# Seven-product pairs that add in one PSUM bank, and 2048-column low parts

## The chip, the cores and the metric

The kernel runs on one core of a Trainium2 chip. The metric is the device time of one execution, in microseconds, as the median over runs. TensorE does the matmuls; VectorE (DVE), ScalarE (ACT) and GpSimd (POOL) do elementwise work; SyncE (SP) issues the loads of weights. Matmul results go to PSUM, which the kernel uses as eight banks of 128 x 512 float32; everything else lives in SBUF.

## The reference

A trunk of two layers for one sequence of 256 tokens, width 1024, in float32. Cut to what matters here:

```python
def hybrid_layer(h, p_i, ...):
    u = rms_norm(h, g_mix_pre)
    (..., gate_a, gate_b) = jnp.split(u @ w_in, offsets, axis=-1)
    branch_a = (o_gla * jax.nn.silu(gg)) @ w_o_gla        # gated linear attention
    branch_b = gqa_attention(q, k, v) @ w_o_attn          # grouped-query attention
    mixed = jax.nn.sigmoid(gate_a) * branch_a + jax.nn.sigmoid(gate_b) * branch_b
    h = h + rms_norm(mixed @ w_out, g_mix_post)

    gate, up = jnp.split(rms_norm(h, g_ffn_pre) @ w_ffn_in, 2, axis=-1)      # 1024 -> 2 x 2816
    h = h + rms_norm((jax.nn.silu(gate) * up) @ w_ffn_out, g_ffn_post)       # 2816 -> 1024

    e = p_i @ w_ple_proj
    return h + rms_norm(jax.nn.sigmoid(h @ w_ple_gate) * e, g_ple_post)
```

## The kernel before

**Precision.** A float32 number is held as a high part and a low part, and each product is made of three matmul passes: high by high, low by high, high by low. `passes` orders them (line 120): for weights as the moving operand it first runs the passes with the high weights for all four blocks of 128 rows, then the four with the low weights. `mm3` (line 104 in the profile) runs the three passes one after the other, so that its second matmul already needs the low weights. A product of 128 tokens by 512 columns over 512 rows is 12 matmuls.

**Weights.** All weights stream from HBM in an order written out beforehand (`plan`), in units of mostly 128 x 2048 float32, 1 MB. `Stream` loads a unit into a raw buffer (two of them, `rawp`; SyncE issues the load at line 294), copies it on ScalarE into the high part `wh` (line 132, in two pieces of 1024 columns) and subtracts that on VectorE from the raw to get the low part `wl` (line 128, in two pieces, each behind its own copy). There are four slots (`wp`) for finished units. `take` hands the next one to the step that uses it; `done` frees it, and `fill` makes the next job's unit.

**Pairs with seven products.** Where a unit of tokens by weights is a 2 x 2 block product (two halves of rows, two of columns), the kernel uses the seven-product form of Strassen and Winograd instead of eight. Per layer there are four such pairs: one in the gate stage (`seven` with `gate_b`) and three in the FFN stage (`pair`, for the blocks `PAIRS`). The sums of the weight blocks are formed in place in lent weight slots: `Stream.step` holds seven steps for a pair, makes a unit at each, and adds two raw blocks at four of them (lines 324, 327, 330, 335, each one 128 x 2048 add on VectorE). x is the running sum in a lent slot, z another lent slot, y a large buffer, q an ordinary raw buffer. `sums` forms the matching sums of the tokens. `seven` (lines 608 to 649) runs the products, `times` each of them, with a `then` behind it that evacuates PSUM: ScalarE copies at lines 635, 638 and 642, a subtract through `vsub` (line 128), and three adds (line 615) once the fifth product is there. Each product except the first two accumulators takes a fresh PSUM bank.

**Order.** The order of a stage is a string. In the gate stage `GATES` mixes u (a unit of the other gate) and m (a unit of an output projection) with the digits of the pair's steps; in the FFN stage `FFN` mixes u (a plain block, `block`), o (a unit of the second FFN matrix, `out_step`) and digits:

```python
FFN = "uu12u34u5u67" "uo12o34o5o67" "poo12o345o67"
GATES = "uuu1u2m34m5m67m"
```

A pair's result is gated, multiplied, and transposed by TensorE some steps later (`turned`, a queue of tasks that count ticks; transposes appear at line 439). Three outs remain for the end of the FFN stage (the stage's tail), where they are run for each half of the tokens. Inside these orders a scheduler places each engine's instructions.

Of the kernel before, what the change touches and what calls it, by code (L numbers as in the profile page):

```python
# [10 lines left out]
F32 = mybir.dt.float32  # L11
# [3 lines left out]
ALU = mybir.AluOpType  # L15
# [43 lines left out]
def trunk_kernel(ctx: ExitStack, tc: tile.TileContext, a: dict, out: bass.AP):  # L59
# [106 lines left out]
    def unit(w, kh, c0):  # L166

        return lambda t: [
            (
                t[:, :2048].rearrange("p (k c) -> p k c", c=512),  # L170
                w[kh * 512 : (kh + 1) * 512, c0 : c0 + 512].rearrange("(k p) c -> p k c", p=P),
            )
        ]
# [25 lines left out]
            )  # L199
        ]  # L200

    plan = []
    for l in range(DEPTH):
        w = a["w_in"][l]
        plan += [unit_rows(w, n, C_RA, C_RA + 1056, FIRST if l + n == 0 else None) for n in range(4)]
        for c0 in (C_AK, C_GQ, C_GK, C_GV, C_GV + 512, C_GG, C_GG + 512):
            plan += [unit(w, kh, c0) for kh in range(2)]
        by_block = lambda w, c: [unit(w, kh, c + j * 512) for j in range(2) for kh in range(2)]
        gates, merges = by_block(w, C_GA), by_block(a["w_o_gla"][l], 0)
        pair = [unit(w, kh, C_GB + j * 512) for kh in range(2) for j in range(2)]  # L210
        for x in GATES:
            plan.append(gates.pop(0) if x == "u" else merges.pop(0) if x == "m" else (pair, int(x)))
        plan += by_block(a["w_o_attn"][l], 0)
        plan += [unit(a["w_out"][l], kh, j * 512) for kh in range(2) for j in range(2)]
        if l == 0:
            plan += [unit_rows(a["w_ple_proj"][l], 0)]
        w = a["w_ffn_in"][l]
        blocks = [[unit_gate_up(w, kh, b) for kh in range(2)] for b in range(NBLK)]
        plan += blocks[0] + blocks[1]
        plains = [u for b in PLAIN for u in blocks[b]]  # L220
        pairs = [[unit(w, kh, c + b * 256) for kh in range(2) for c in (0, HIDDEN)] for b in PAIRS]
        outs = [unit_rows(a["w_ffn_out"][l], n) for n in OUT]
        for x in FFN.replace("p", ""):
            if x == "1":
                pair = pairs.pop(0)
            plan.append(plains.pop(0) if x == "u" else outs.pop(0) if x == "o" else (pair, int(x)))
        plan += outs
        plan += [unit(a["w_ple_gate"][l], kh, j * 512) for kh in range(2) for j in range(2)]
        if l + 1 < DEPTH:
            plan += [unit_rows(a["w_ple_proj"][l + 1], 0)]  # L230

    class Load:


        def __init__(self, make, own=None, waits=False):
            self.make, self.own, self.waits, self.raw, self.n = make, own, waits, None, 0

        def start(self):
            if self.own:
# [5 lines left out]
    class Stream:  # L245
# [8 lines left out]
        def __init__(self, depth):  # L254
            self.depth, self.held, self.room, self.ready, self.open = depth, 0, 0, [], False
            self.loads, self.jobs, self.lend = [], [], False
            pairs = {}
            for item in plan:
                if callable(item):
                    x = Load(item)  # L260
                    self.loads.append(x)
                    self.jobs.append(lambda x=x: self.plain(x))
                else:
                    units, n = item
                    if n == 1:
                        b11, b12, b21, b22 = units
                        x, z = (Load(b, lambda tag=tag: self.lent(tag), tag == "wh") for b, tag in ((b11, "wh"), (b12, "wl")))
                        y, q = Load(b22, big), Load(b21)
                        pairs[id(units)] = x, y, z, q
                        self.loads += [x, y, z]  # L270
                    if n == 5:
                        self.loads.append(q)
                    self.jobs.append(lambda p=pairs[id(units)], n=n: self.step(n, *p))

# [36 lines left out]
            return self.jobs.pop(0)()  # L311

        def plain(self, x):
            return self.put(x)

        def made(self, x):
            for piece in self.put(x):
                split(*piece)

        def step(self, n, x, y, z, q):  # L320
            c = slice(0, 2048)
            if n == 1:
                self.made(x)
                nc.vector.tensor_tensor(out=x.raw[:, c], in0=x.raw[:, c], in1=z.raw[:, c], op=ALU.add)
            elif n == 2:
                self.made(y)
                nc.vector.tensor_tensor(out=z.raw[:, c], in0=z.raw[:, c], in1=y.raw[:, c], op=ALU.add)
            elif n == 3:
                self.made(x)
                nc.vector.tensor_tensor(out=x.raw[:, c], in0=x.raw[:, c], in1=y.raw[:, c], op=ALU.add)  # L330
            elif n == 4:
                self.made(z)
            elif n == 5:
                self.made(x)
                nc.vector.tensor_tensor(out=x.raw[:, c], in0=x.raw[:, c], in1=q.raw[:, c], op=ALU.add)
            elif n == 6:
                self.made(q)
            else:
                self.load()
                self.made(x)  # L340
                self.held -= 1
                self.lend = True

        def fill(self):
            while self.open and self.held < self.depth and self.jobs:
# [259 lines left out]

        return made, Task(make(), part[0])

    def seven(sp, forms, gated):

        made, task = forms  # L610
        quad = lambda hf, j: lambda k: sp.tok(4 * j + k, hf)
        form = lambda i: lambda k: [p[:, k, :] for p in made[i]]

        def add(out, x, y):
            nc.vector.tensor_tensor(out=out, in0=x, in1=y, op=ALU.add)

        (p1, v), (p3, p7) = (halves(mid()) for _ in range(2))
        c11, p5, o = acc(), acc(), []
        c12, c22 = p3, p7

        def product(i, then):

            o[:] = [acc()]
            times(o[0], form(i), True, then)

        def both():
            add(v, o[0], v)
            add(c12, v, p3)
            add(c22, v, p7)

        def last():
            vsub(v, p5, c22)
            gated(1, v, c22)

        times(c11, quad(0, 0), True, lambda: nc.scalar.copy(p1, c11))
        yield
        task.need()
        product(0, lambda: nc.scalar.copy(p3, o[0]))
        yield
        times(p5, form(1), True, lambda: vsub(v, p5, p1))  # L640
        yield
        product(2, lambda: nc.scalar.copy(p7, o[0]))
        yield
        product(3, both)
        yield
        times(c11, quad(0, 1), False, lambda: gated(0, c11, c12))
        yield
        times(p5, quad(1, 1), False, last)
        yield

    def project_t(sp):
# [232 lines left out]
    for l in range(DEPTH):  # L884
# [404 lines left out]
        def sigmoid(br, hf, j, src):  # L1289
            if sgate[br] is None:  # L1290
                sgate[br] = big().rearrange("p (s c) -> p s c", s=2)
            with tc.issue_after(last_exp[0].ins):
                nc.scalar.activation(sgate[br][:, hf, j * 512 : (j + 1) * 512], src, AF.Sigmoid)

        def blocks(sp, then):

            for j in range(2):
                o = [acc(), acc()]
                for kh in range(2):
                    w = ws.take()  # L1300
                    for hf in range(2):
                        amode(o[hf], sp, hf, kh * 4, w, kh == 0, kh == 1)
                    if kh == 1:
                        for hf in range(2):
                            then(j, hf, o[hf])
                    ws.done()
                    yield
# [16 lines left out]
        def merge(br):  # L1324
# [15 lines left out]
        steps = {  # L1340
            "u": blocks(uT, lambda j, hf, o: sigmoid(0, hf, j, o)),
            "m": blocks(gT, merge(0)),
            "s": seven(uT, forms, gate_b),
        }
        for x in GATES:
            if x == "m":
# [44 lines left out]
        for hf in range(2):  # L1391
            ws.lend = hf == 1
            for b in range(2):
                o = acc()
                for kh in range(2):
                    amode(o, u2, hf, kh * 4, us[b][kh], kh == 0, kh == 1, fresh=b == 0)
                sg = t512()
                nc.scalar.activation(sg[:, 0:256], o[:, 0:256], AF.Silu)
                vmul(sg[:, 0:256], o[:, 256:512], sg[:, 0:256])
                turned(sg[:, 0:256], 2 * b, 2, hf)  # L1400
                if hf == 1:
                    ws.done(2)
                if (hf, b) == (1, 0):
                    forms = sums(plain)
# [32 lines left out]
        def pair(b):  # L1437
            def gated(hf, gate, up):
                sg = t512()
                nc.scalar.activation(sg, gate, AF.Silu)  # L1440
                vmul(sg, up, sg)
                turned(sg, 2 * b, 4, hf, WAIT_LAST[hf] if b == PAIRS[-1] else WAIT_PAIR)

            return seven(u2, forms, gated)

        o = []

# [135 lines left out]
```

## Time and profile before

| | |
|---|---|
| median of 3 runs | 924.27 us (923.92 to 924.66) |
| profiled execution, first to last instruction | 922.9 us |
| matmuls and transposes on TensorE | busy 912.2 us, 99%, 4668 records |
| weight loads on TensorE | busy 776.2 us, 84% |
| VectorE | busy 786.1 us, 85%, 1002 instructions |
| ScalarE | busy 578.5 us, 63%, 954 instructions |
| GpSimd | busy 83.8 us, 9% |
| HBM read | 169.50 MB; 187 GB/s over the span |

The runs' time stands 1.4 us above the profiled span (924.27 - 922.9). In the profile, PE is the matmul part of TensorE, PEld its weight loads, L with a number a line of the kernel, and names such as `acc_0ffnin` a tile of layer 0's FFN stage. An entry "2.36 ... x2" in the timeline is two instructions back to back. The text in square brackets behind a row is the engine's idle time before it and what ended it.

### The profile page before, as it was taken

The numbers are of one execution on the slowest core, as the hardware profiler recorded it, in microseconds if no ns is written. First come the engines' busy times: TensorE is split into PE (matmuls) and PEld (weight loads), VectorE is DVE, ScalarE is ACT, GpSimd is POOL, SyncE is SP. The second block draws the span as 40 slices with busy tenths as digits, with TensorE's granted clock in tenths as the row PEclk, the third lists the DMA queues.
The fourth block names the chain that finished last, engine by engine and source line by source line (L and its number), as shares of the span: only waits on it lengthen the run. The fifth ranks groups of instructions, "written<-read, shape, count | busy, mean of one in ns | idle before, by whom it ended". The sixth has DMA issues, their size and how long they took to land.

```text
span 922.9 us, 12406 instructions
## 1 busy us (share of the span) xinstructions
PE 912.2 (99%) x4668; PEld 776.2 (84%) x4668; DVE 786.1 (85%) x1002; ACT 578.5 (63%) x954; POOL 83.8 (9%) x147
## 2 busy tenths in 40 slices
PE   9999999999999999999999999999999999999996
PEld 6898888888888888888899988888888888888885
DVE  6898989987579998999779789798875799989884
ACT  4669676664567656566676677765644766565563
POOL 3400211300000000000114001100001000000000
PEclk9999999999999999999999999999999999999999
DMA  7463455656286565647576424454573756545361
GB/s 260 144 230 134 148 173 188 201 193 232 90 277 222 178 233 168 265 128 268 188 256 220 153 92 137 137 191 174 195 260 104 268 177 204 223 177 217 126 239 45
DMA packets 88679, 173.44 MB, mean 188 GB/s; under 512 B 3422, under 2 KB 26470, under 8 KB 88108
## 3 DMA queue, kind: packets, MB, share of 16 engines
q1 hardware_dynamic: 88460, 172.40, 54.0%
q8 instruction: 36, 0.59, 0.3%
q10 hardware_dynamic: 160, 0.27, 0.1%
q14 instruction: 23, 0.19, 0.1%
HBM read 169.50 MB, written 3.15 MB: 187 GB/s over the span
## 4 chain that ended last, share of the span: by engine, by line
PE 94%; DVE 2%; ACT 1%; DMA 1%; issue 1%; POOL 0%; POOLq 0%; DVEq 0%; ACTq 0%; SPq 0%
PE acc_0ffnin L120 12%; PE acc_1ffnin L120 11%; PE acc_1gate L120 7%; PE acc_0gate L120 7%; PE acc_0ffnin L104 7%; PE acc_1ffnin L104 7%; PE acc_1rq L120 3%; PE acc_0gqk L120 2%; PE acc_0wout L120 2%; PE acc_1gqk L120 2%; PE acc_1ple L120 2%; PE acc_0ple L120 2%; PE acc_0gg L120 2%; PE acc_1gg L120 2%; PE acc_0v L120 2%; PE acc_1merge L120 2%
## 5 line engine op out<-in xcount | busy, mean ns | idle before, releaser
L104 PE MATMUL acc_0ffnin<-wh_0ffnin,big_0ffnin 128*128 128x512 f32 x176 | 56.9, 393 | 0.0
L104 PE MATMUL acc_1ffnin<-wh_1ffnin,big_1ffnin 128*128 128x512 f32 x176 | 56.8, 392 | 0.0
L132 ACT CAST wh_1ffnin<-raw_1ffnin 128x1024 fp32r<-128x1024 f32 x38 | 38.5, 1049 | 27.3 <-DMA raw_1ffnin<-in_w_ffn_out_dram 8.7
L132 ACT CAST wh_0ffnin<-raw_0ffnin 128x1024 fp32r<-128x1024 f32 x38 | 38.4, 1048 | 23.8 <-PE acc_0ffnin L120 7.8
L128 DVE TENSOR_TENSOR wl_1ffnin<-raw_1ffnin,wh_1ffnin 128x1024 fp32r<-128x1024 f32 x38 | 45.0, 1221 | 8.9 <-ACT wh_1ffnin L132 8.9
L128 DVE TENSOR_TENSOR wl_0ffnin<-raw_0ffnin,wh_0ffnin 128x1024 fp32r<-128x1024 f32 x38 | 44.8, 1220 | 7.1 <-ACT wh_0ffnin L132 7.0
L120 PE MATMUL acc_1ffnin<-wh_1ffnin,big_1wout 128*128 128x512 f32 x168 | 42.5, 393 | 0.0
L120 PE MATMUL acc_0ffnin<-wh_0ffnin,big_0wout 128*128 128x512 f32 x168 | 42.5, 393 | 0.0
L104 PEld LDWEIGHTS acc_0ffnin<-wh_0ffnin,big_0ffnin 128*128 128x128 f32 x176 | 33.0, 188 | 7.1 <-DVE big_0ffnin L128 0.5
L104 PEld LDWEIGHTS acc_1ffnin<-wh_1ffnin,big_1ffnin 128*128 128x128 f32 x176 | 33.1, 188 | 6.7
L128 DVE TENSOR_TENSOR wl_1ffnin<-lent_1ffnin,wh_1ffnin 128x1024 fp32r<-128x1024 f32 x30 | 35.8, 1218 | 1.7 <-ACT wh_1ffnin L132 1.7
L128 DVE TENSOR_TENSOR wl_0ffnin<-lent_0ffnin,wh_0ffnin 128x1024 fp32r<-128x1024 f32 x30 | 35.8, 1216 | 1.7 <-ACT wh_0ffnin L132 1.7
L120 PEld LDWEIGHTS acc_1ffnin<-wh_1ffnin,big_1wout 128*128 128x128 f32 x168 | 31.1, 188 | 6.2
L120 PEld LDWEIGHTS acc_0ffnin<-wh_0ffnin,big_0wout 128*128 128x128 f32 x168 | 31.1, 188 | 6.2
L132 ACT CAST wh_1ffnin<-lent_1ffnin 128x1024 fp32r<-128x1024 f32 x30 | 30.7, 1053 | 7.1 <-PE acc_1ffnin L104 3.9
L132 ACT CAST wh_0ffnin<-lent_0ffnin 128x1024 fp32r<-128x1024 f32 x30 | 30.7, 1054 | 6.7 <-PE acc_0ffnin L104 3.9
L104 PE MATMUL acc_0ffnin<-wl_0ffnin,big_0ffnin 128*128 128x512 f32 x88 | 34.3, 389 | 0.0
L104 PE MATMUL acc_1ffnin<-wl_1ffnin,big_1ffnin 128*128 128x512 f32 x88 | 34.3, 389 | 0.0
L128 DVE TENSOR_TENSOR wl_1gate<-raw_1gate,wh_1gate 128x1024 fp32r<-128x1024 f32 x20 | 23.6, 1219 | 5.4 <-ACT wh_1gate L132 5.3
L128 DVE TENSOR_TENSOR wl_0gate<-raw_0gate,wh_0gate 128x1024 fp32r<-128x1024 f32 x20 | 23.7, 1226 | 4.8 <-ACT wh_0gate L132 4.8
L132 ACT CAST wh_0gate<-raw_0gate 128x1024 fp32r<-128x1024 f32 x20 | 20.0, 1048 | 11.7 <-DMA raw_0gate<-in_w_o_attn_dram 5.6
L132 ACT CAST wh_1gate<-raw_1gate 128x1024 fp32r<-128x1024 f32 x20 | 20.0, 1049 | 11.5 <-DMA raw_1gate<-in_w_o_attn_dram 5.5
(695 smaller groups left out, 2691.8 us busy)
## 6 DMA issues: line engine op xcount, KB each, us to landing
raw_0ffnin<-in_w_ffn_out_dram SPq DMA_DIRECT2D x11, 1024.0 KB, 6.6
raw_1ffnin<-in_w_ffn_out_dram SPq DMA_DIRECT2D x11, 1024.0 KB, 5.1
lent_0ffnin<-in_w_ffn_in_dram SPq DMA_DIRECT2D x6, 1024.0 KB, 7.4
lent_1ffnin<-in_w_ffn_in_dram SPq DMA_DIRECT2D x6, 1024.0 KB, 8.3
raw_0v<-in_w_in_dram SPq DMA_DIRECT2D x4, 1024.0 KB, 4.9
raw_0gate<-in_w_o_gla_dram SPq DMA_DIRECT2D x4, 1024.0 KB, 4.9
raw_0gate<-in_w_o_attn_dram SPq DMA_DIRECT2D x4, 1024.0 KB, 5.1
raw_0wout<-in_w_ffn_in_dram SPq DMA_DIRECT2D x8, 512.0 KB, 4.9
```

The source lines that it names most:

```text
L104: return nc.tensor.matmul(o, lhsT, rhs, start=start, stop=stop)
L120: nc.tensor.matmul(o, x, y, start=start and n == 0, stop=stop and n == len(seq) - 1, **kw)
L128: nc.vector.tensor_tensor(out=out, in0=in0, in1=in1, op=ALU.subtract)
L132: nc.scalar.copy(hi, src)
```

## The change

It changes two things.

First, the units of the pairs, of the plain FFN blocks and of the second FFN matrix are put on a list `wide`. For them ScalarE still makes the high part in two copies of 1024 columns, but VectorE makes the low part in one subtract of 2048 columns, after both copies.

Second, `seven` is written anew. The order of the products changes, and one PSUM bank (`bank`, the first accumulator of the stage, kept for all of its pairs) takes the sum of several products: VectorE writes p5 - p1 into it, product 3 is added to it by the matmuls, ScalarE copies the sum out (u4), product form0 is added, ScalarE copies that out as c12 and writes u4 back, and form2 is added; c21 is then one subtract. The three adds of the old `seven` are not there any more; two ScalarE copies per pair are new. `Stream.step` makes the units in the new order: q is loaded and used at step 3 instead of 5 and 6, its raw buffer is given back at step 4 instead of 7, and the slots for the next pair are lent after step 6.

```diff
--- before.py
+++ after.py
@@ -199,7 +199,7 @@
             )
         ]
 
-    plan = []
+    plan, wide = [], []
     for l in range(DEPTH):
         w = a["w_in"][l]
         plan += [unit_rows(w, n, C_RA, C_RA + 1056, FIRST if l + n == 0 else None) for n in range(4)]
@@ -208,6 +208,7 @@
         by_block = lambda w, c: [unit(w, kh, c + j * 512) for j in range(2) for kh in range(2)]
         gates, merges = by_block(w, C_GA), by_block(a["w_o_gla"][l], 0)
         pair = [unit(w, kh, C_GB + j * 512) for kh in range(2) for j in range(2)]
+        wide += pair
         for x in GATES:
             plan.append(gates.pop(0) if x == "u" else merges.pop(0) if x == "m" else (pair, int(x)))
         plan += by_block(a["w_o_attn"][l], 0)
@@ -216,10 +217,12 @@
             plan += [unit_rows(a["w_ple_proj"][l], 0)]
         w = a["w_ffn_in"][l]
         blocks = [[unit_gate_up(w, kh, b) for kh in range(2)] for b in range(NBLK)]
+        wide += [u for b in PLAIN for u in blocks[b]]
         plan += blocks[0] + blocks[1]
         plains = [u for b in PLAIN for u in blocks[b]]
         pairs = [[unit(w, kh, c + b * 256) for kh in range(2) for c in (0, HIDDEN)] for b in PAIRS]
         outs = [unit_rows(a["w_ffn_out"][l], n) for n in OUT]
+        wide += [u for units in pairs for u in units] + outs
         for x in FFN.replace("p", ""):
             if x == "1":
                 pair = pairs.pop(0)
@@ -234,6 +237,7 @@
 
         def __init__(self, make, own=None, waits=False):
             self.make, self.own, self.waits, self.raw, self.n = make, own, waits, None, 0
+            self.wide = make in wide
 
         def start(self):
             if self.own:
@@ -268,7 +272,7 @@
                         y, q = Load(b22, big), Load(b21)
                         pairs[id(units)] = x, y, z, q
                         self.loads += [x, y, z]
-                    if n == 5:
+                    if n == 3:
                         self.loads.append(q)
                     self.jobs.append(lambda p=pairs[id(units)], n=n: self.step(n, *p))
 
@@ -311,35 +315,49 @@
             return self.jobs.pop(0)()
 
         def plain(self, x):
+            if x.wide:
+                self.made(x)
+                return self.load()
             return self.put(x)
 
         def made(self, x):
-            for piece in self.put(x):
-                split(*piece)
+            pieces = self.put(x)
+            if not x.wide:
+                for piece in pieces:
+                    split(*piece)
+                return
+            for hi, _, src in pieces:
+                nc.scalar.copy(hi, src)
+            wh, wl = (t[:, : x.n] for t in self.ready[-1])
+            vsub(wl, x.raw[:, : x.n], wh.bitcast(F32))
 
         def step(self, n, x, y, z, q):
-            c = slice(0, 2048)
+            def add(to, b):
+                c = slice(0, 2048)
+                nc.vector.tensor_tensor(out=to.raw[:, c], in0=to.raw[:, c], in1=b.raw[:, c], op=ALU.add)
             if n == 1:
                 self.made(x)
-                nc.vector.tensor_tensor(out=x.raw[:, c], in0=x.raw[:, c], in1=z.raw[:, c], op=ALU.add)
+                add(x, z)
             elif n == 2:
+                self.made(x)
+                add(x, y)
+            elif n == 3:
+                self.made(q)
+            elif n == 4:
+                self.made(x)
+                add(x, q)
+                self.load()
+            elif n == 5:
                 self.made(y)
-                nc.vector.tensor_tensor(out=z.raw[:, c], in0=z.raw[:, c], in1=y.raw[:, c], op=ALU.add)
-            elif n == 3:
-                self.made(x)
-                nc.vector.tensor_tensor(out=x.raw[:, c], in0=x.raw[:, c], in1=y.raw[:, c], op=ALU.add)
-            elif n == 4:
-                self.made(z)
-            elif n == 5:
-                self.made(x)
-                nc.vector.tensor_tensor(out=x.raw[:, c], in0=x.raw[:, c], in1=q.raw[:, c], op=ALU.add)
+                add(z, y)
             elif n == 6:
-                self.made(q)
-            else:
-                self.load()
                 self.made(x)
                 self.held -= 1
                 self.lend = True
+                self.start()
+            else:
+                self.made(z)
 
         def fill(self):
             while self.open and self.held < self.depth and self.jobs:
@@ -605,47 +623,41 @@
 
         return made, Task(make(), part[0])
 
-    def seven(sp, forms, gated):
+    def seven(sp, forms, gated, bank):
 
         made, task = forms
         quad = lambda hf, j: lambda k: sp.tok(4 * j + k, hf)
         form = lambda i: lambda k: [p[:, k, :] for p in made[i]]
-
-        def add(out, x, y):
-            nc.vector.tensor_tensor(out=out, in0=x, in1=y, op=ALU.add)
-
-        (p1, v), (p3, p7) = (halves(mid()) for _ in range(2))
-        c11, p5, o = acc(), acc(), []
-        c12, c22 = p3, p7
-
-        def product(i, then):
-
-            o[:] = [acc()]
-            times(o[0], form(i), True, then)
-
-        def both():
-            add(v, o[0], v)
-            add(c12, v, p3)
-            add(c22, v, p7)
+        (p1, u4), (c12, c21) = (halves(mid()) for _ in range(2))
+        c11, p5 = acc(), acc()
+        def upper():
+            nc.scalar.copy(c12, bank[0])
+            nc.scalar.copy(bank[0], u4)
+            gated(0, c11, c12)
 
         def last():
-            vsub(v, p5, c22)
-            gated(1, v, c22)
+            vsub(c21, p1, bank[0])
+            gated(1, c21, bank[0])
 
         times(c11, quad(0, 0), True, lambda: nc.scalar.copy(p1, c11))
         yield
         task.need()
-        product(0, lambda: nc.scalar.copy(p3, o[0]))
+        times(p5, form(1), True, lambda: vsub(bank[0], p5, p1))
         yield
-        times(p5, form(1), True, lambda: vsub(v, p5, p1))
+        times(c11, quad(0, 1), False)
         yield
-        product(2, lambda: nc.scalar.copy(p7, o[0]))
+        times(bank[0], form(3), False, lambda: nc.scalar.copy(u4, bank[0]))
         yield
-        product(3, both)
+        times(bank[0], form(0), False, upper)
         yield
-        times(c11, quad(0, 1), False, lambda: gated(0, c11, c12))
+        times(p5, quad(1, 1), False, lambda: nc.scalar.copy(p1, p5))
         yield
-        times(p5, quad(1, 1), False, last)
+        times(bank[0], form(2), False, last)
         yield
 
     def project_t(sp):
@@ -1292,10 +1304,14 @@
             with tc.issue_after(last_exp[0].ins):
                 nc.scalar.activation(sgate[br][:, hf, j * 512 : (j + 1) * 512], src, AF.Sigmoid)
 
+        bank = []
         def blocks(sp, then):
 
             for j in range(2):
                 o = [acc(), acc()]
+                if not bank:
+                    bank.append(o[0])
                 for kh in range(2):
                     w = ws.take()
                     for hf in range(2):
@@ -1340,7 +1356,7 @@
         steps = {
             "u": blocks(uT, lambda j, hf, o: sigmoid(0, hf, j, o)),
             "m": blocks(gT, merge(0)),
-            "s": seven(uT, forms, gate_b),
+            "s": seven(uT, forms, gate_b, bank),
         }
         for x in GATES:
             if x == "m":
@@ -1392,6 +1408,8 @@
             ws.lend = hf == 1
             for b in range(2):
                 o = acc()
+                if not hf + b:
+                    bank = [o]
                 for kh in range(2):
                     amode(o, u2, hf, kh * 4, us[b][kh], kh == 0, kh == 1, fresh=b == 0)
                 sg = t512()
@@ -1441,7 +1459,7 @@
                 vmul(sg, up, sg)
                 turned(sg, 2 * b, 4, hf, WAIT_LAST[hf] if b == PAIRS[-1] else WAIT_PAIR)
 
-            return seven(u2, forms, gated)
+            return seven(u2, forms, gated, bank)
 
         o = []
 
```

## The prediction

> **What bounds the kernel now.** I first read the page for the shares, then the chain of waits, then busy time by stretch.
>
> ```profile
> PE 912.2 (99%) x4668; PEld 776.2 (84%) x4668; DVE 786.1 (85%) x1002; ACT 578.5 (63%) x954; POOL 83.8 (9%) x147
> PEclk9999999999999999999999999999999999999999
> PE 94%; DVE 2%; ACT 1%; DMA 1%; issue 1%; POOL 0%; POOLq 0%; DVEq 0%; ACTq 0%; SPq 0%
> ```
>
> TensorE is busy for 912.2 of 922.9 us at full clock and carries 94% of the chain that ended last. VectorE, at 85%, carries 2%. As TensorE's busy time uses modelled ends, I check it by stretches and by start-to-start pace. Columns: busy us and count of PE, PEld, DVE, ACT, POOL, then clock, DMA share, GB/s.
>
> ```profile
> 0.00:156.00 156.00, 153.22 (x901) 134.24 (x901) 135.21 (x240) 107.00 (x229) 32.32 (x60) 1.00 0.55 188
> 284.00:330.00 46.00, 46.00 (x210) 38.08 (x209) 43.98 (x44) 29.23 (x39) 0.00 (x0) 1.00 0.56 190
> 330.00:380.00 50.00, 50.00 (x228) 41.44 (x227) 45.65 (x44) 30.03 (x36) 0.95 (x1) 1.00 0.59 213
> 380.00:440.00 60.00, 59.97 (x276) 49.43 (x275) 55.72 (x54) 37.92 (x50) 0.87 (x2) 1.00 0.58 201
> 666.00:722.00 56.00, 55.87 (x281) 46.72 (x280) 39.06 (x48) 30.22 (x47) 4.50 (x9) 1.00 0.52 175
> 722.00:757.00 35.00, 34.90 (x163) 28.82 (x163) 31.76 (x38) 22.31 (x36) 0.00 (x0) 1.00 0.69 230
> 892.00:923.00 31.00, 23.45 (x130) 20.25 (x129) 16.95 (x28) 10.75 (x23) 2.69 (x6) 0.93 0.18 67
> ```
>
> The first FFN stage, where most of the change lies, is 284 to 440. TensorE is idle there for 0.03 of 156 us, although VectorE is busy for 93% of it (43.98 + 45.65 + 55.72 = 145.35 us). What idle time exists lies at the start (2.78 us to 156) and the end (7.55 us after 892), where the changed steps don't run. The chain, started in the gate stage, in a pair, and near the end:
>
> ```profile
> 156.24 51.71 PE acc_0gate L120 x228
> 396.56 5.44 PE acc_0ffnin L104 x24
> 402.00 8.16 PE acc_0ffnin L120 x36
> 410.16 5.44 PE acc_0ffnin L104 x24
> 424.68 0.03 issue
> 892.45 6.80 PE acc_1ple L120 x30
> ```
>
> 51.71/228 = 226.8 ns per matmul, 8.16/36 = 226.7, and 6.80/30 = 226.7 in the late stretch where VectorE has 16.95 us of work in 31. The pace doesn't depend on how full VectorE is, and the pieces join end to end. So each of the pair's 12-matmul steps is 2.72 us, and the time is a count of matmuls times this pace plus ends. The change can win only from waits that aren't there.
>
> **The change, part by part.**
>
> *Matmuls.* Each pair keeps seven products of 12 matmuls; only their order and target banks differ, and both built programs hold the same number of matmuls and transposes. DMAs are equal in number too. Cost 0.
>
> *Wide low parts.* 45 units a layer (7 in gates, 27 of FFN in, 11 outs), 90 in all, replace two subtracts by one.
>
> ```profile
> L132 ACT CAST wh_0ffnin<-raw_0ffnin 128x1024 fp32r<-128x1024 f32 x38 | 38.4, 1048 | 23.8 <-PE acc_0ffnin L120 7.8
> L128 DVE TENSOR_TENSOR wl_0ffnin<-raw_0ffnin,wh_0ffnin 128x1024 fp32r<-128x1024 f32 x38 | 44.8, 1220 | 7.1 <-ACT wh_0ffnin L132 7.0
> L335 DVE TENSOR_TENSOR lent_0ffnin<-lent_0ffnin,raw_0ffnin 128x2048 f32<-128x2048 f32 x3 | 6.9, 2290 | 0.1
> 402.08 2.00 ACT L132 CAST wh_0ffnin<-lent_0ffnin 128x1024 fp32r<-128x1024 f32 x2 [3.87 <-PE acc_0ffnin L104]
> 403.16 2.36 DVE L128 TENSOR_TENSOR wl_0ffnin<-lent_0ffnin,wh_0ffnin 128x1024 fp32r<-128x1024 f32 x2 [1.67 <-ACT wh_0ffnin L132]
> ```
>
> No 2048-column subtract is in the trace; the nearest row is the 2048-column add, 2.29 us. Two subtracts back to back take 2.36 us, so a unit saves 0.07 us of elapsed VectorE time, or 2 x 1.22 - 2.29 = 0.15 by the means: 6 to 14 us in all, off TensorE's path. Against it stands latency. The subtract now waits for both copies: counted from the first copy's start, the whole low part comes at 2.00 + 2.29 = 4.3 us instead of 3.4 (403.16 + 2.36 - 402.08), and its first half 2.0 us later than at 1.05 + 1.22 = 2.3. In `passes` the low weights come only after two thirds of a step's matmuls, 8 x 0.227 = 1.8 us in, which pays for that. In `out_step` the second matmul already needs them. The exposed units are outs whose low part comes just in time:
>
> ```profile
> 408.00 1.05 ACT L132 CAST wh_0ffnin<-raw_0ffnin 128x1024 fp32r<-128x1024 f32 x1
> 408.24 4.63 DVE L128 TENSOR_TENSOR wl_0ffnin<-raw_0ffnin,wh_0ffnin 128x1024 fp32r<-128x1024 f32 x4
> 878.00 2.00 ACT L132 CAST wh_1ffnin<-raw_1ffnin 128x1024 fp32r<-128x1024 f32 x2 [0.77 <-DMA raw_1ffnin<-in_w_ffn_out_dram]
> 879.08 2.36 DVE L128 TENSOR_TENSOR wl_1ffnin<-raw_1ffnin,wh_1ffnin 128x1024 fp32r<-128x1024 f32 x2 [1.13 <-ACT wh_1ffnin L132]
> 880.46 0.40 PE L104 MATMUL acc_1ffnin<-wl_1ffnin,big_1ffnin 128*128 128x512 f32 x1
> ```
>
> In the third pair the out unit's copies end at 409.05, and TensorE starts that unit at 410.16: a wide subtract would end at 409.1 + 2.29 = 411.4, 1.0 us past its second matmul (410.16 + 0.23). In layer 1's tail, copies end at 880.0, the wide subtract at 882.35, against a use at 880.46: 1.9 us. With supply unchanged that is 2.9 us a layer. But supply changes: the step that adds q now comes fourth, not fifth, its raw buffer goes back at step 4 instead of 7 (3 x 2.72 = 8.2 us sooner) and SP's later loads move up with it.
>
> ```profile
> raw_0ffnin<-in_w_ffn_out_dram SPq DMA_DIRECT2D x11, 1024.0 KB, 6.6
> raw_1ffnin<-in_w_ffn_out_dram SPq DMA_DIRECT2D x11, 1024.0 KB, 5.1
> ```
>
> At 5 to 7 us from issue to landing, 8 us of head start covers the 1.9 us in the tail; the third pair's case also sheds the add in front of it. Bounds 0 to 2.9 us a layer; I take 0.2, near the covered end.
>
> *Fewer adds.* Three `add`s per pair go, 24 in 8 pairs; two ScalarE copies per pair come, 16.
>
> ```profile
> L615 DVE TENSOR_TENSOR mid_0ffnin<-mid_0ffnin,mid_0ffnin 128x512 f32<-128x512 f32 x6 | 3.9, 684 | 0.0
> L635 ACT COPY mid_0ffnin<-acc_0ffnin 128x512 f32<-128x512 f32 x3 | 1.7, 581 | 0.0
> ```
>
> VectorE loses 24 x 0.68 = 16 us, ScalarE gains 16 x 0.58 = 9.3 us. Together VectorE falls to about 756 to 764 us, ScalarE rises to about 588. Neither is on the path: worth 0 to 0.3 us a layer at most, the 0.23 us that TensorE idles in 666 to 757 being the largest sum in a stretch with pairs. I take none.
>
> *One bank in series.* This adds waits. Before, every product had its own PSUM bank and its evacuation ran under the next product. Now product 3 waits for VectorE's seed of the bank, form0 for ScalarE's copy of u4 out of it, form2 for two ScalarE copies (c12 out, u4 in), and the next pair's seed for `last`. Behind a waiting matmul everything on TensorE stands. Cover per hand-off: seed under c11's second half (2.72 us) against 0.68 of work plus at most one wide subtract, 2.97; form2 under quad(1,1), 2.72 against 2 x 0.58 plus at most two copies, 3.16; form0 in the third pair has no step between, only four out matmuls that the scheduler sets there, 4 x 0.227 = 0.91 us, against 0.58 plus at most one copy of 1.05, 1.63. So 0 to 0.25, 0 to 0.45, 0 to 0.72 us, plus semaphore trips. One trip shows in these rows:
>
> ```profile
> 405.44 0.68 DVE L128 TENSOR_TENSOR mid_0ffnin<-acc_0ffnin,mid_0ffnin 128x512 f32<-128x512 f32 x1
> 407.53 0.57 ACT L642 COPY mid_0ffnin<-acc_0ffnin 128x512 f32<-128x512 f32 x1
> ```
>
> Products end at 402.00 + 24 x 0.2267 = 407.44; the copy starts 0.09 us later. ScalarE is busy 63% of the stage, so the third pair's form0 meets a running copy more often than not: I take 0.3 us a layer there, 0.1 for the other hand-offs, and 0.1 for a gated unit that comes earlier. The Trainium skill ("Perfetto Trace Analysis", section "Matmuls") speaks against this part: independent matmul groups should rotate through PSUM banks so that evacuation overlaps the next group. By that rule alone, each uncovered evacuation would cost its 0.58 us; the row above agrees as far as the old kernel hides its copies, and no row shows a shared bank.
>
> **Sum.** Per layer 0.2 + 0.3 + 0.1 + 0.1 = 0.7, two layers 1.4 us. Profiled span 922.9 + 1.4 = 924.3; the median of the runs, 924.27, lies 1.4 above the span, so **925.7 us**, +1.4.
>
> A measurement of this kernel can tell about 0.2%, 1.85 us, from no change.
>
> **The rivals.**
>
> *A, the forecast: TensorE-bound as before, 0 to 1.8 us of new waits.* 924.3 to 926.1.
>
> *B, slower: the shared bank paces the pairs.* If the queues were full at every hand-off, each of 8 pairs would wait 0.25 + 0.45 and some four trips of 0.09, and the two third pairs 0.72 more: 8 x 1.06 + 1.44 = 9.9 us. With ScalarE busy for 63% and bursts that seldom meet, I expect a fifth to two fifths of it, 2 to 4 us: 926.3 to 928.3. It decides from the point at which the work queued ahead of a hand-off passes its 2.72 us step. For: VectorE's units are now single blocks of 2.3 us, and it was 93% busy. Against: it loses three operations a pair.
>
> *C, slower: the wide low part is late for outs.* If the earlier loads don't help, 2 x 2.9 = 5.8 us, plus A's other terms 1.0: 931.1. For: the rows at 408.24 and 879.08. Against: the 8.2 us head start.
>
> *D, faster: VectorE is the true bound.* If TensorE's full share were an artefact and VectorE set the time, the 22 us that it loses at least (6 + 16) would come off: 902. Against: the equal pace at full and light VectorE load, and at most 0.23 us of idle starts in a stretch with pairs; chance 0.01. The Trainium skill ("Perfetto Trace Analysis", section "Identifying the Most-Contended Engine") holds that TensorE's busy share misleads and that its weight-load share be used instead. That is 84% here, which would put VectorE's 85% first; by that rule the trace does not agree, since the pace is the measure. A small form has 0.08: VectorE's relief and the earlier loads bring the last stage forward into the 7.55 us that TensorE idles after 892, by 2 to 3 us: 921.3 to 922.3. Against: the joined pieces before and after 892.45 show no load waited for.
>
> That the change moves nothing because VectorE is no bound is A with zero waits.
>
> **How the numbers follow.** A 0.50, B 0.33, C 0.08, D 0.09. So same 0.50, slower 0.41, faster 0.09. The range takes A and most of B: 923.6 (a gain of 0.7, three times 0.23) to 928.6 (the top of B with 0.3 for run spread), leaving out C, D and B's edge, about 0.2 in all. A's own range is 924.3 to 926.1.
>
> **What would show it.** VectorE busy near 760 with some 114 instructions fewer, ScalarE near 588, TensorE's pace still 226.7 ns. For A, the pieces of the chain in the FFN stages join with gaps summing below 2 us. For B, starts of form0 or form2 matmuls released by ScalarE's copies, or of product 3 by VectorE's seed. For C, `out_step` matmuls in the third pair and the tail released by a 2048-column subtract. For D, a shorter stretch from the first FFN matmul to the last with no fewer matmuls. The forecast is wrong if TensorE's idle time in those stretches grows by over 2 us, or if a stretch with equal matmul count gets shorter by more than 0.3 us.

## The result, and the profile after

The changed kernel takes 932.45 us (median of 4 runs, 930.4 to 933.35) against 924.38 us before: ratio 1.008, interval 1.0068 to 1.0092. By the medians it is slower by 8.1 us (6.3 to 8.5 by the interval), and 932.45 lies above the range of the prediction (923.6 to 928.6). The page of the changed kernel, busy time by engine and the chain's shares:

```profile
PE 914.4 (98%) x4668; PEld 777.8 (84%) x4668; DVE 766.7 (82%) x888; ACT 586.2 (63%) x970; POOL 83.3 (9%) x147
PE 90%; DVE 4%; DMA 2%; ACT 2%; issue 1%; POOL 0%; SPq 0%; POOLq 0%; DVEq 0%; ACTq 0%
```

The work moved much as costed: VectorE lost 114 instructions and 19 us, ScalarE gained 16 and 8 us, TensorE has the same 4668 records. But TensorE's share of the chain fell from 94% to 90%, and the span grew from 922.9 to 930.5 us. TensorE's waits in the changed kernel (total us, times, longest) say where. Those of the kernel's start are left out: the longest two, 1.6 and 1.4 us, were 1.6 and 0.4 before, and the gate stage begins no later for it. The longest that remain:

```profile
PE aux_0ffnout L457 <- DVE h L555: 4.1, 1, 4.1
PE acc_1ffnin L104 <- DVE wl_1ffnin L128: 0.3, 1, 0.3
PE acc_0ffnin L120 <- DVE wl_0ffnin L128: 0.3, 1, 0.3
```

One wait of 4.1 us stands out, in layer 0's FFN tail, where TensorE transposes the new h. The two waits on a wide low part, which the prediction had feared, are 0.3 us each. The chain of the changed kernel through that place, and then the chain of before at the same transposes (L457 after, L439 before):

```profile
427.84 8.21 PE acc_0ffnin L104 x36
...
439.55 1.22 DVE mid_0ffnin L128
440.77 0.03 issue
440.80 0.75 DVE mid_0ffnout L125 x2
441.55 0.45 issue
442.00 0.75 DVE h L555
442.75 0.14 issue
442.89 1.94 PE aux_0ffnout L457 x8
444.83 7.09 PE acc_0ple L120 x23
```

```profile
427.70 6.84 PE acc_0ffnin L104 x30
434.54 0.88 PE aux_0ffnout L439 x8
435.41 4.11 PE acc_0ffnin L104 x18
439.52 8.39 PE acc_0ple L120 x37
```

Before, h is there in time, and 18 matmuls of outs still lie behind its transposes. Afterwards all 36 matmuls are done first, and TensorE then stands until 442.89. The post-norm's multiply (`mid_0ffnout`, L125) begins at 440.80, right behind an instruction that has nothing to do with it: `mid_0ffnin` L128, the low part of the next layer's decay weights, 17 rows, made in `up_weights`. VectorE's timeline of the changed kernel around it:

```profile
429.83 0.68 DVE L128 TENSOR_TENSOR big_0ffnin<-aux_0ffnin,big_0ffnin 128x512 fp32r<-128x512 f32 x1
434.44 2.36 DVE L128 TENSOR_TENSOR wl_0ffnout<-raw_0ffnin,wh_0ffnout 128x1024 fp32r<-128x1024 f32 x2 [3.93 <-ACT wh_0ffnout L132]
437.16 2.36 DVE L128 TENSOR_TENSOR wl_0ffnout<-raw_0ffnin,wh_0ffnout 128x1024 fp32r<-128x1024 f32 x2 [0.36 <-ACT wh_0ffnout L132]
439.55 1.22 DVE L128 TENSOR_TENSOR mid_0ffnin<-mid_0ffnin,mid_0ffnin 17x1024 fp32r<-17x1024 f32 x1
440.80 1.29 DVE L125 TENSOR_TENSOR mid_0ffnout<-acc_0ffnin,mid_0ffnin 128x512 f32<-128x512 f32 x2
```

VectorE idles for 3.93 us from 430.51, while the multiply's PSUM input is complete: ScalarE squares it from 430.01 on. Before, the decay weights' subtract and the same multiply ran so:

```profile
419.84 1.22 DVE L128 TENSOR_TENSOR mid_0ffnin<-mid_0ffnin,mid_0ffnin 17x1024 fp32r<-17x1024 f32 x1
431.70 1.28 DVE L125 TENSOR_TENSOR mid_0ffnout<-acc_0ffnin,mid_0ffnin 128x512 f32<-128x512 f32 x2
```

The multiply now stands in the queue behind the low parts of two later units and of the decay weights, and VectorE does not take it ahead of them. The decay weights' subtract comes 20 us later. What comes late ahead of it is their small loads on SP. Rows of SP's queue around the last small load (line 718 before, 730 after), before and then after:

```profile
394.18 0.37 SPq L294 DMA_DIRECT2D raw_0ffnin<-in_w_ffn_out_dram  x1
396.48 0.28 SPq L718 DMA_DIRECT2D mid_0ffnin<-in_b_alpha_dram  x1
410.62 8.98 SPq L294 DMA_DIRECT2D raw_0ffnin<-in_w_ffn_out_dram  x3
```

```profile
396.72 12.51 SPq L298 DMA_DIRECT2D raw_0ffnin<-in_w_ffn_out_dram  x3
409.32 0.42 SPq L729 DMA_DIRECT2D mid_0ffnin<-in_w_alpha_up_dram  x1
427.67 2.65 SPq L298 DMA_DIRECT2D raw_0ffnin<-in_w_ple_gate_dram  x2
430.38 0.35 SPq L730 DMA_DIRECT2D mid_0ffnin<-in_b_alpha_dram  x1
```

In the new step order three raw loads come ahead of the six small loads and stand in SP's queue until 409, waiting for raw buffers. The small loads then go out between further raw loads, the last at 430.38 instead of 396.48. When ScalarE copies the decay weights (437.98), the copy comes right behind another one and no wait for a load shows: its place in the queue, and the subtract's on VectorE, was set when the program was built. That the late loads put them there is read from the order of the queues; the experiments test it.

The wait has an echo. Busy time and clock by stretch, in the changed kernel (the eighth figure is the granted clock):

```profile
438.50:442.80 4.30, 0.25 (x2) 0.00 (x0) 4.24 (x6) 2.63 (x6) 1.08 (x2) 0.85 1.00 370
442.80:448.20 5.40, 5.31 (x16) 4.38 (x17) 5.37 (x8) 2.32 (x4) 0.00 (x0) 0.50 1.00 404
448.20:460.00 11.80, 11.80 (x59) 9.82 (x58) 5.05 (x8) 4.87 (x8) 0.00 (x0) 0.99 0.42 147
```

After 4 us without matmuls TensorE runs at a clock of 0.50 for 5.4 us: eight transposes take 1.94 us instead of 0.88, and 512-column matmuls start 0.43 us apart instead of 0.227.

### The profile page after: what moved, and what is told of

Its sections match the earlier page's. It is cut to its first block, busy times and chain, and to the rows that moved or that the text cites. A ratio compares the mean times of both kernels' runs of the same rounds, so it can differ in the third digit from the quotient of the medians.

```text
span 930.5 us, 12320 instructions
## 1 busy us (share of the span) xinstructions
PE 914.4 (98%) x4668; PEld 777.8 (84%) x4668; DVE 766.7 (82%) x888; ACT 586.2 (63%) x970; POOL 83.3 (9%) x147
## 4 chain that ended last, share of the span: by engine, by line
PE 90%; DVE 4%; DMA 2%; ACT 2%; issue 1%; POOL 0%; SPq 0%; POOLq 0%; DVEq 0%; ACTq 0%
PE acc_0ffnin L120 10%; PE acc_1ffnin L120 10%; PE acc_1gate L120 7%; PE acc_0gate L120 7%; PE acc_0ffnin L104 6%; PE acc_1ffnin L104 6%; PE acc_0ple L120 3%; PE acc_1rq L120 2%; PE acc_0gqk L120 2%; PE acc_0wout L120 2%; PE acc_1gqk L120 2%; PE acc_1ple L120 2%; PE acc_1gg L120 2%; PE acc_0gg L120 2%; PE acc_0v L120 2%; PE acc_0merge L120 2%
## 5 line engine op out<-in xcount | busy, mean ns | idle before, releaser
L128 DVE TENSOR_TENSOR wl_0ffnin<-raw_0ffnin,wh_0ffnin 128x2048 fp32r<-128x2048 f32 (+1 forms) x20 | 43.0, 2180 | 7.6 <-ACT wh_0ffnin L330 7.5
L128 DVE TENSOR_TENSOR wl_1ffnin<-raw_1ffnin,wh_1ffnin 128x2048 fp32r<-128x2048 f32 (+1 forms) x20 | 43.1, 2180 | 6.6 <-ACT wh_1ffnin L330 6.5
L330 ACT CAST wh_0ffnin<-raw_0ffnin 128x1024 fp32r<-128x1024 f32 x36 | 36.5, 1049 | 18.0 <-DMA raw_0ffnin<-in_w_ffn_in_dram 6.4
L330 ACT CAST wh_1ffnin<-raw_1ffnin 128x1024 fp32r<-128x1024 f32 x36 | 36.5, 1049 | 17.1 <-DMA raw_1ffnin<-in_w_ffn_out_dram 6.0
L128 DVE TENSOR_TENSOR wl_1ffnin<-lent_1ffnin,wh_1ffnin 128x2048 fp32r<-128x2048 f32 x15 | 34.3, 2286 | 8.2 <-ACT wh_1ffnin L330 5.1
L128 DVE TENSOR_TENSOR wl_0ffnin<-lent_0ffnin,wh_0ffnin 128x2048 fp32r<-128x2048 f32 x15 | 34.3, 2286 | 7.6 <-ACT wh_0ffnin L330 4.5
L128 DVE TENSOR_TENSOR wl_0gate<-raw_0gate,wh_0gate 128x1024 fp32r<-128x1024 f32 (+1 forms) x19 | 24.3, 1318 | 5.7 <-ACT wh_0gate L132 5.6
L128 DVE TENSOR_TENSOR wl_1gate<-raw_1gate,wh_1gate 128x1024 fp32r<-128x1024 f32 (+1 forms) x19 | 23.5, 1277 | 4.8 <-ACT wh_1gate L132 4.7
```

What stands on the lines that cost most here:

```text
L128: nc.vector.tensor_tensor(out=out, in0=in0, in1=in1, op=ALU.subtract)
L330: nc.scalar.copy(hi, src)
```

## The experiments

Three theories stood against each other. Q: the small loads come late on SP, so that other work stands behind them in VectorE's queue, and half clock adds to the wait. B: the shared bank paces the pairs. C: wide low parts come late for outs. The kernel before, measured beside each group, took 924.42, 924.48 and 925.07 us.

**Small loads early (e1).** `up_weights` is written out ahead of the third pair.

```diff
+                if l + 1 < DEPTH:
+                    wup_next = up_weights(l + 1)      # in the loop over FFN, at "p"
...
-        if l + 1 < DEPTH:
-            wup_next = up_weights(l + 1)              # after the loop
```

> The changed kernel, with up_weights (six small loads, a ScalarE copy and a 17-row VectorE subtract for the next layer's decay weights) written out at the mark p, ahead of the third pair, instead of after the FFN loop. Theory Q (queue order): the six small loads sit behind raw weight loads on SP, so their low part comes late on VectorE, stands ahead of the post-norm's multiply in VectorE's queue, and TensorE waits 4.1 us for h in layer 0's tail, then runs some 2 us slower at half clock. Q expects the wait at the transposes of h to go: 932.4 - 4.3 - 2.1 = 926.0 us, within 925 to 926.5. Rival B (the shared bank paces the pairs) and rival C (wide low parts late for the outs) expect no change: 931.5 to 933.

925.95 us, ratio 1.0017 (1.0008 to 1.0026). The post-norm's multiply runs on time again:

```profile
430.12 1.43 DVE L125 TENSOR_TENSOR mid_0ffnout<-acc_0ffnin,mid_0ffnin 128x512 f32<-128x512 f32 x2
433.96 1.03 PE L457 MATMUL aux_0ffnout<-ident,h 128*128 128x128 f32 x8
```

The time is within the 925 to 926.5 that Q expected; B and C expected no difference. With both of its parts in place, the change then measures 1.5 us, so the place of `up_weights` is worth 6.5 of the 8.1 us. The kernel before was not run with the same move.

**The bank without wide low parts (e3).** `self.wide = make in wide` becomes `self.wide = False`.

> The changed kernel with the list of wide units ignored: all low parts in two subtracts of 1024 columns, the new seven with its shared bank kept. Q expects the same wait in layer 0's tail, since SP's order of loads comes from the new step order: 931 to 933 us. B expects the same time for another reason, with waits at the shared bank inside the pairs. C expects 924 to 925 us.

930.48 us, ratio 1.0068 (1.0055 to 1.008), with the same wait of 4.1 us for h at the same place. Wide low parts aren't needed for the loss. It comes with the new `seven` and its order of steps. The time is just under the 931 to 933 that Q expected, and 2.0 us under the changed kernel: the slow stretch behind the wait is shorter here (last section).

**Filler matmuls in the wait (e5).** Nineteen spare matmuls keep TensorE busy; the results are unused.

```diff
+            if l == 0:
+                if hf == 0:
+                    spare = acc()
+                    mm(spare, keep[:, 0:P], keep, True, True)
+                else:
+                    for _ in range(18):
+                        mm(spare, keep[:, 0:P], keep, True, True)
             post_norm_add(o[hf], gpost, hf)
```

> The changed kernel with 18 spare 512-column matmuls (4.1 us, results unused) set on TensorE between the last out and the transposes of h in layer 0's tail, and one more ahead of the tail's second half. VectorE's queue is as in the changed kernel, so h is as late. If the half clock after the wait comes from TensorE idling, the clock stays full and the time falls by about 2.1 less 0.2 us: 930.5 us. If the clock drops there for another reason, the time stays at 932.4 to 932.7 us.

929.81 us, 2.6 us less than the changed kernel, though it does more; 930.5 was expected if idling is the cause. The filler, the transposes behind it, and the two stretches after:

```profile
438.78 4.06 PE L104 MATMUL acc_0ffnout<-keep 128*128 128x512 bf16 x18
442.99 1.32 PE L457 MATMUL aux_0ffnout<-ident,h 128*128 128x128 f32 x8
```

```profile
438.50:443.00 4.50, 4.35 (x21) 1.71 (x20) 4.44 (x7) 2.80 (x6) 1.07 (x2) 1.00 0.97 350
443.00:448.00 5.00, 4.60 (x22) 3.57 (x23) 5.00 (x8) 2.14 (x4) 0.00 (x0) 1.00 1.02 411
```

The transposes come as late as before the edit (442.99 against 442.89), and the clock stays at 1.00. So the half clock is due to the idle time and costs some 2.6 us of the 8.1. The changed kernel's own rows give the same size: 1.1 us for the transposes (1.94 - 0.88) and some 1.6 for the eight matmuls behind them (8 x 0.2). The Trainium skill ("TensorE: Matmul & The Clock Gate", section "What's actually happening") says that TensorE falls to half rate after an idle window of about 3.4 us, in windows that run freely. The trace agrees: 4.1 us without matmuls, a clock of 0.50 and 0.43 us from start to start.

**Wide low parts without the bank (e4).** The kernel before, with the list `wide` and the new `made`.

> The kernel before with only the wide low parts: the old seven with its own banks and its old step order. Q expects 924.5 to 926 us: no late alpha loads, some tenths of waits where a wide low part comes late. C expects nearly all of the loss here: 930 to 932 us. B expects 924.4 us.

928.32 us, ratio 1.0038 (1.0026 to 1.0051): a miss for Q, and half of what C expected. In layer 1's tail:

```profile
874.79 2.29 DVE L128 TENSOR_TENSOR wl_1ffnin<-raw_1ffnin,wh_1ffnin 128x2048 fp32r<-128x2048 f32 x1 [2.97 <-ACT wh_1ffnin L330]
877.14 0.50 PE L104 MATMUL acc_1ffnin<-wl_1ffnin,big_1ffnin 128*128 128x512 f32 x1 [1.43 <-DVE wl_1ffnin L128]
```

This is C's mechanism at C's place: the out's second matmul waits 1.43 us for the end of one wide subtract, where 1.9 was predicted. In the old order C is real.

**Small loads after the tail (e2).** In the changed kernel, `up_weights` moves behind the tail's post-norms.

> The changed kernel with up_weights written out after the tail's post-norms: its six small loads stay late, but its 17-row subtract no longer stands ahead of the post-norm's multiply on VectorE. If the order of VectorE's queue is what makes h late, the wait goes as with the early loads: 925 to 927 us. If the loss comes from the late loads themselves (or their DMA traffic in the tail), the wait stays: 930 us or more.

932.51 us, ratio 1.0085 (1.0071 to 1.0098). The wait for h is gone, and the time is the same:

```profile
PE acc_0ple L120 <- ACT big_0ffnout L132: 2.2, 1, 2.2
PE aux_1emb L869 <- DMA mid_0ffnout<-in_p_dram: 1.5, 1, 1.5
```

```profile
447.26 0.39 SPq L861 DMA_DIRECT2D mid_0ffnout<-in_p_dram  x1
451.36 1.06 ACT L731 CAST mid_0ffnout<-mid_0ffnout 81x1024 fp32r<-81x1024 f32 x1 [7.88 <-DMA mid_0ffnout<-in_b_alpha_dram]
```

Now the load of p stands behind the small loads on SP, and the copies of h's transposes behind the decay weights' copy on ScalarE, which idles 7.88 us for the last small load. My expectation asked only for VectorE's order; what counts is that the loads are late, and whichever queue they come to stops.

**The old kernel with late small loads (g3).** The same move in the kernel before, and nothing else.

> The kernel before, with up_weights written out after layer 0's tail and nothing else changed: no shared bank, no wide low parts, no new step order. Its built order has the six small loads behind the raw loads on SP and ahead of the load of p, as in the changed kernel with late loads. If late small loads in the in-order queues are enough by themselves, TensorE waits behind ScalarE's copy and the load of p after layer 0's tail, as there: 928 to 932 us. If it takes the new seven or the wide low parts to lose time, 924.4 us.

933.16 us, ratio 1.0086 (1.0073 to 1.01), above the 928 to 932 expected:

```profile
PE aux_1emb L857 <- DMA mid_0ffnout<-in_p_dram: 3.0, 1, 3.0
PE acc_0ple L120 <- ACT big_0ffnout L132: 2.2, 1, 2.2
```

No shared bank, no wide low part, no new step: late small loads alone cost as much as the whole change. The waits are those of e2, one stage on from the wait of the changed kernel.

**The bank alone, small loads early (f1).** e1 and e3 together.

> The changed kernel with all low parts in two subtracts of 1024 columns and up_weights at the mark p: the new seven with its shared bank, alone. Q expects the shared bank to cost nothing that can be told: 924 to 925.3 us. Rival B (the bank paces the pairs) expects 926.3 to 928.3 us.

925.2 us, ratio 1.0009 (1.0 to 1.0017), within what Q expected: B falls as a mechanism of 2 to 4 us. The hand-off named in the prediction, form0 of the third pair behind the copy of u4 (L654), does show in the chain:

```profile
406.85 1.05 ACT wh_0ffnin L132
407.91 0.49 ACT mid_0ffnin L654
408.40 0.04 issue
408.44 3.01 PE acc_0ffnin L120 x12
```

The copy ran right behind a high-part copy of 1.05 us; twelve matmuls take 3.01 instead of 2.72 us.

**Outs narrow, small loads early (f3).** e1 with `+ outs` taken off `wide`.

> The changed kernel with up_weights at the mark p and the 11 outs a layer taken off the list of wide units; pair and plain units stay wide. If what is left of the loss (925.95 with wide outs) is the late low part of outs, the time falls to 924.3 to 925.2 us. If it lies in the pairs, it stays at about 926 us.

925.31 us, ratio 1.0009 (1.0 to 1.0017). It is 0.6 us less than e1 and just above the 924.3 to 925.2 of "outs"; the intervals overlap, so this only leans towards outs as the rest.

**Wide low parts in the old kernel, by kind (f4, f7).** f4 is e4 with `+ outs` taken off the list; f7 has outs alone on it.

> The kernel before with wide low parts for pair and plain units, not for outs. Wide low parts everywhere cost 3.9 us in the old order (928.32). C in the form of the prediction says that outs carry that, because out_step's second matmul needs the low part: 924.3 to 925.3 us here. If the longer block on VectorE's queue is what costs, most of the loss stays: 927 us or more.

> The kernel before with wide low parts for the 11 outs a layer alone. The prediction's C said that outs are where a late low part costs, 2.9 us a layer with supply unchanged (as here): 930.1 us. The trace with all units wide shows waits at such outs of 0.5 us in layer 0 and 1.6 us in layer 1, so C corrected to those gives 926.0 to 927 us. If outs carry nothing, 924.4 us.

f4 took 928.22 us, ratio 1.0042 (1.0028 to 1.0055); f7 took 927.85 us, ratio 1.003 (1.0018 to 1.0042), between its two forecasts for outs (926 to 927, and 930.1). Longest waits behind the kernel's start, of f7 (whose profile is of its slowest run, 929.88) and then of f4:

```profile
PE acc_0ffnin L104 <- DVE wl_0ffnin L128: 1.2, 1, 1.2
PE acc_1ffnin L104 <- DVE wl_1ffnin L128: 1.1, 2, 0.6
```

```profile
PE aux_0ple L454 <- DVE mid_0ple L512: 1.9, 1, 1.9
```

Outs alone cost 2.8 us, at outs, by C. Pair and plain units alone cost 3.7 us, and their main wait is in a stage that no wide unit belongs to. The two don't add: together they cost 3.9. f4 was a miss for C's form "outs carry it all". In f4's trace the transposes of p (`aux_1emb`) stand behind 44 matmuls of layer 0's last stage instead of 37 and start at 449.60 instead of 447.91 us, so TensorE's own order differs ahead of the late norm. What changed that order, and whether it is the whole cause, wasn't tried.

## Why the prediction was wrong

**What bounds the kernel** was right. TensorE's pace is the same (5.44 us for 24 matmuls, 226.7 ns), VectorE's 19 us bought nothing, and D falls with that.

**The step that failed** is the one on supply: "its raw buffer goes back at step 4 instead of 7 (3 x 2.72 = 8.2 us sooner) and SP's later loads move up with it". I counted this as cover for the outs and did not ask what those loads move past. Six small loads stand in the same queue. The last now goes out 34 us later (430.38 against 396.48), and the subtract made from them comes 20 us later on VectorE (439.55 against 419.84), in front of a multiply that the diff does not touch. No term of the sum and none of the rivals held this. Its size is 932.45 - 925.95 = 6.5 us: the wait and its half clock. The sum has terms only for the changed steps, but the order of the queues is made from the whole program.

**The idle clock** was missing too. I priced waits at their length; a wait of 4.1 us cost some 2.6 more.

**The terms that were walked** came out smaller than priced. That the sum for them, +1.4 us, is close to the +1.5 measured with the small loads early (925.95 against 924.42) is partly luck. The profiled executions, in us from the first matmul into one tile to the first into the next:

| Stretch | before | changed | e1 | f1 |
|---|---|---|---|---|
| layer 0, gate and FFN stages with the tail (`acc_0gate` to `acc_0ple`) | 298.1 | 303.8 | 298.1 | 298.3 |
| layer 0, last stage (`acc_0ple` to `acc_1rq`) | 29.8 | 31.7 | 29.8 | 29.8 |
| layer 1, first projections (`acc_1rq` to `acc_1kv`) | 24.8 | 24.5 | 25.5 | 25.5 |
| layer 1, gate and FFN stages with the tail (`acc_1gate` to `acc_1ple`) | 292.7 | 293.4 | 293.2 | 292.8 |

Rows one and four hold all pairs and wide units. There the shared bank alone (f1) adds 0.3 us, against 1.0 in the sum (0.5 a layer for hand-offs and the gated unit); the one wait that shows is at the predicted place. Bank and wide low parts together (e1) add 0.5 us, against 1.4. The wide low parts, put at 0.2 a layer, show waits of 0.3 us in each layer of the changed kernel. Another 0.7 us of e1 and f1 lies in row three, where no pair and no wide unit runs. ScalarE waits for a weight load there, in e1 (second row) and not before (first):

```profile
469.23 2.06 ACT L132 CAST wh_0ple<-raw_0ple 128x1056 fp32r<-128x1056 f32 x2
470.10 2.05 ACT L132 CAST wh_0ple<-raw_0ple 128x1056 fp32r<-128x1056 f32 x2 [1.42 <-DMA raw_0ple<-in_w_in_dram]
```

The three kernels with the small loads early (e1, f1, f3) show 25.5 to 25.8 us in this row, the seven that leave `up_weights` in its place (before, changed, e3, e4, e5, f4, f7) 24.5 to 24.9. In these profiles, then, this part goes with the moved loads, not with the bank or the low parts.

Rival C, priced at 5.8 us without the earlier loads, measures 2.8 for outs in the old order: the mechanism was right, the price double. VectorE came to 766.7 us, just above the 756 to 764 given, though the wide subtract takes 2.29 us as its nearest row said; where the difference lies is not shown.

**Left open**: why pair and plain units alone cost 3.7 us in the old order, and why a weight load comes later in layer 1's first projections once the small loads are early. That the earlier steps for q are what lets three raw loads ahead of the small ones is read from the two orders on SP; no run moved q by itself.

## What to carry to other kernels

In a kernel whose main engine is full, the queues of all the others are schedules: when a change moves a load or a step, list everything else in the same in-order queue, also small work for a later stage, and follow each to its last consumer. Here small loads that went out up to 34 us late cost 6.5 us, and 114 instructions saved brought nothing. Before blaming the new code, undo the move by itself: here it separated 6.5 us of order from 1.5 us of everything else. Then look at where the rest lies: about half of it was not in the changed steps either.

## What the runs showed of the hardware that I had not expected

After a single idle stretch of 4.1 us TensorE's clock was 0.50 for 5.4 us, and 18 useless matmuls in that gap made the kernel 2.6 us faster. The half-clock stretch isn't of one length: with the same 4.1 us wait in e3, the clock over the next 3.7 us was 0.58, and 0.97 over the 4.8 us behind that:

```profile
441.50:445.20 3.70, 3.31 (x12) 2.78 (x13) 3.70 (x7) 2.53 (x4) 0.00 (x0) 0.58 1.02 397
```
